# Numerators of the windowed attention: the low part is multiplied with the high part of the values only

## The chip, the cores and the metric

The kernel runs on one core of a Trainium2 chip. The core has a matrix engine (TensorE, here PE, with its weight loads shown apart as PEld), a vector engine (VectorE, DVE), a scalar engine (ScalarE, ACT), a general engine (GpSimd, POOL), and a queue engine (SyncE, SP) that issues nearly all of this kernel's transfers to 16 DMA engines. The metric is the device time of one execution in microseconds; a kernel's time is the median of its runs.

## The reference

One inference step of a one-layer decoder: a normalized input is projected into the parts of two mixers, a dilated sliding-window attention (8 heads of 64) and a gated linear attention (GLA, 4 heads), whose gated outputs go through one output projection. There are 2048 prompt tokens and 64 sample tokens (8 sequences of 8). The change touches the prompt's attention. Its three branches have the windows and dilations (128, 1), (512, 4) and (2048, 16); each is softmax attention over blocks of 128 queries, with the current and the previous block of 128 keys:

```python
DILATED = ((128, 1), (512, 4), (2048, 16))
BAND_BLOCK = 128

def softmax_attend(s, v, out_spec):
    m = jnp.max(s, axis=-1, keepdims=True)
    p = jnp.exp(s - m)
    den = jnp.sum(p, axis=-1)
    o = jnp.einsum(out_spec, p, v) / den[..., None]
    return o, m[..., 0] + jnp.log(den)

def dilated_branch_prompt(q, k, v, window, dil):
    ...
    s = jnp.einsum('brnqhd,brnkhd->brnqhk', qr, kk) * (hd ** -0.5)
    s = jnp.where(valid[None, None, :, :, None, :], s, -jnp.inf)
    o, lse = softmax_attend(s, vv, 'brnqhk,brnkhd->brnqhd')
    ...

def dilated_mixture(results):
    outs = jnp.stack([r[0] for r in results], axis=0)
    lses = jnp.stack([r[1] for r in results], axis=0)
    alpha = jax.nn.softmax(lses, axis=0)
    return jnp.einsum('gblh,gblhd->blhd', alpha, outs)
```

The numerators of the title are the sums of `p` times `v` before the division.

## The kernel before

**Numbers in two parts.** Products that need more than a 16-bit float holds are made of float16 pairs: a value is written as a high part (its rounding to float16) and a low part (the rest, again float16). In the input projections (`project`, L1761) three products are added: high by high, high by low, low by high. In the attention, the values of each head are stored with 64 high columns beside 64 low columns, so that a block of values for one head is a 128x128 tile; the exponentials `p` are split into a high and a low 128x128 block as well (`split`, L1003 to L1016).

**One unit of attention** is made by `attend` (L1018) from four steps. `pre` loads queries, keys and values. `qk` makes scores on PE (L1031, tiles `s`), then DVE adds the mask and finds the extreme (L1039) and ACT takes the exponential (L1042) into tiles `p`. `tr` transposes `p` in float32 through PE (L1049, tiles `t`), and `split` makes the two parts `pt`: one unit in two goes over ACT (L1008) and DVE (L1009), the others over ACT (L1011 and L1013) or DVE (L1015) and POOL (L1016). `pv` multiplies on PE: for each head `i` and each key block `b`, first the high part (`c` = 0) and then the low part (`c` = 1) of `pt` is loaded as weights, and the 128 columns of values are streamed through it into the PSUM tile `O` (L1064). The 128 columns of one head in `O` thus end as 64 columns of sums with the high values and 64 with the low values; `post` calls `added` (L1075 to L1081), in which ACT copies the second half out and DVE adds the first half to it. There are 600 such pairs of products, 1200 matmuls: two key blocks in most units of the branches of dilation 1 and 4 (`unit`), one in the branch of dilation 16 (`branch3`).

**What runs beside it.** From about 153 us to 735 us of the span these units are interleaved on PE with the projections of the input (values, queries, keys, then the GLA's query, key, value and gate blocks). Behind that come the GLA itself, the attention of the sample tokens, and the output projection (L2120). On POOL and DVE, dot products of the cached keys with the sample queries run beside the prompt's attention (L1616, L1617); their keys come in by DMA.

**Order.** The order of the instructions on every engine is written out: a table of numbers per engine, applied by `in_order` (L675), sets for each engine which instruction follows which. Waits between engines are semaphores that follow from the data.

Of the kernel before, what the change touches and what calls it, by code (L numbers as in the profile page):

```python
# [18 lines left out]
P = 128  # L19
# [3 lines left out]
HD = 64  # L23
# [667 lines left out]
def tile_hymba(ctx: ExitStack, tc: tile.TileContext, A: dict):  # L691
# [277 lines left out]
    with ExitStack() as c1:  # L969
# [33 lines left out]
        def split(out, in_, f):  # L1003

            split_[0] += 1
            h, l = out
            if split_[0] % 2:
                ACT.activation(h, in_, AF.Copy, scale=P_SCALE)  # L1008
                DVE.scalar_tensor_tensor(l, in_, P_SCALE, h, ALU.mult, ALU.subtract)  # L1009
            else:  # L1010
                ACT.activation(f, in_, AF.Copy, scale=P_SCALE)  # L1011
                if split_[0] % 4:
                    ACT.activation(h, f, AF.Copy)  # L1013
                else:
                    DVE.tensor_copy(h, f)  # L1015
                POOL.tensor_tensor(l, f, h, ALU.subtract)  # L1016

        def attend(tag, nh, nb, scores, mask, vf, nmf, denf, OT, pre=None, post=None, neg=-1.0):  # L1018

            w = nb * P
            t = {}

            def qk():
                s_ps = ps_S.tile([P, 512], F32, name=f"s_{tag}", tag="S")
                s = t["s"] = sp.tile([P, 512], F32, name=f"p_{tag}", tag="s")
                for i in range(nh):
                    prods = scores(i)
                    for n, (q, k) in enumerate(prods):  # L1030
                        PE.matmul(  # L1031
                            s_ps[:, i * w : (i + 1) * w], q, k,
                            start=(n == 0), stop=(n == len(prods) - 1),
                        )
                    if nh == 2 or i % 2:
                        yield
                for i in range(nh):
                    sl = slice(i * w, (i + 1) * w)
                    DVE.tensor_tensor_reduce(  # L1039
                        s[:, sl], s_ps[:, sl], mask, neg, BIG, ALU.add, ALU.min, nmf(i)  # L1040
                    )
                    ACT.activation(  # L1042
                        s[:, sl], s[:, sl], AF.Exp, bias=nmf(i), scale=-1.0, accum_out=denf(i)
                    )

            def tr():
                p_ps = ps_P.tile([P, 512], F32, name=f"t_{tag}", tag="PT")
                for i in range(nh * nb):
                    PE.transpose(  # L1049
                        p_ps[:, i * P : (i + 1) * P], t["s"][:, i * P : (i + 1) * P], ident[:]  # L1050
                    )
                    if i == 1:
                        yield
                pt = t["pt"] = ptp.tile([P, 2, 512], F16, name=f"pt_{tag}", tag="pt")
                w_ = slice(0, nh * w)
                split([pt[:, c, w_] for c in range(2)], p_ps[:, w_], t["s"][:, w_])
                yield

            def pv():
                for i in range(nh):  # L1060
                    o_ = OT(i)
                    for n in range(2 * nb):
                        b, c = divmod(n, 2)
                        PE.matmul(  # L1064
                            o_, t["pt"][:, c, (i * nb + b) * P : (i * nb + b + 1) * P], vf(i, b),
                            start=(n == 0), stop=(n == 2 * nb - 1),
                        )
                    if nh == 2 or i % 2:
                        yield
                if post:  # L1070
                    post()

            return [pre, qk, tr, pv]
# [602 lines left out]
        for nm_, src in (("q", A["q_norm_w"]), ("k", A["k_norm_w"])):  # L1676
            i = "qk".index(nm_)
# [210 lines left out]
        for i in range(3):  # L1888
            for lst, nm_ in ((st["qbd"], "qbd"), (Sbd, "Sbd"))[: 2 if i < 2 else 1]:
                t = gst.tile([P, 2, 256], F32, name=f"{nm_}{i}")  # L1890
# [644 lines left out]
```

## Time and profile before

| | us |
|---|---|
| median of 3 runs | 1231.39 (1228.66 to 1232.98) |
| the profiled execution, its own time | 1232.75 |
| its span, first to last instruction | 1230.7 |
| DVE busy in the span | 916.5 |
| ACT busy in the span | 826.2 |
| POOL busy in the span | 539.2 |

The profile shows one execution. An engine's busy time is the union of its instructions' times; a group of instructions is shown by source line, with count, busy time and the mean duration of one. The matmul's duration runs from its start to its modelled end, and several matmuls are under way at once, so durations of matmuls can't be added up: from the start of one to the start of the next is less. A chain of waits follows the work back from the last instruction and shows for each piece how far the time advanced; for a run of matmuls that is start to start. A weight load (PEld) stands in a row of its own and lies beside the matmuls.

### The profile page before, as it was taken

What the parts mean: (1) busy time and instruction counts of PE and PEld (TensorE: products, weight loads), DVE (VectorE), ACT (ScalarE), POOL (GpSimd) and SP (SyncE); (2) the same over time, 40 slices, a digit from 0 to 9 for tenths busy, and PEclk for the clock granted to TensorE, in tenths of its full rate; (3) what the DMA queues carried; (4) which work ended last, traced back from release to release, by engine and by line L of the source; (5) the groups of instructions that cost most, each with busy time, mean ns of one, the idle gap of its engine ahead of it and who ended that gap; (6) DMA issues with size and microseconds to landing.
All of it is one profiled execution on the core that took longest, in us unless ns stands there. A gap on an engine that the chain in (4) does not pass through costs nothing.

```text
span 1230.7 us, 26121 instructions
## 1 busy us (share of the span) xinstructions
PE 1174.5 (95%) x8942; PEld 717.4 (58%) x8942; DVE 916.5 (74%) x2457; ACT 826.2 (67%) x2189; POOL 539.2 (44%) x478
## 2 busy tenths in 40 slices
PE   3899999999999899998999999999999999999998
PEld 1444475566566556765777676645546665555543
DVE  5888687888878957777778665678888999743562
ACT  7656598789779968987777554577788864521220
POOL 0054444565547335553354467755544454311220
PEclk9999999999999999999999999999999999999999
DMA  7488956777955897799999978956673287999962
GB/s 260 161 235 217 235 186 152 204 218 193 228 175 169 202 270 220 258 241 284 275 245 265 250 232 222 267 167 224 223 227 103 95 266 254 320 367 403 385 223 77
DMA packets 235832, 283.07 MB, mean 230 GB/s; under 512 B 116194, under 2 KB 146867, under 8 KB 232627
## 3 DMA queue, kind: packets, MB, share of 16 engines
q1 hardware_dynamic: 235698, 281.40, 76.7%
q8 instruction: 71, 1.16, 0.4%
q14 instruction: 63, 0.51, 0.1%
HBM read 183.02 MB, written 75.24 MB: 210 GB/s over the span
## 4 chain that ended last, share of the span: by engine, by line
PE 45%; DVE 8%; ACT 4%; DMA 3%; issue 2%; POOL 1%; SPq 1%; ACTq 0%; POOLq 0%; DVEq 0%
PE Y L2120 11%; PE acc_g L1761 6%; PE acc_vb L1761 5%; PE acc_qkb L1761 4%; PE acc_gb L1761 4%; PE OS L2377 2%; PE O L1064 2%; PE t L1049 2%; PE s L1031 2%; PE sc_e L875 1%; DMA o_d<-o 1%; PE tm L2085 1%; DVE kq_e L846 1%; DVE Sbd L1940 1%; ACT qbd L834 1%
## 5 line engine op out<-in xcount | busy, mean ns | idle before, releaser
L1761 PEld LDWEIGHTS <-hr 128*128 128x128 f16 x1824 | 171.4, 98 | 103.5 <-issue 12.0
L1616 POOL TENSOR_TENSOR pr<-k,qb 128x512 f32<-128x512 f32 x128 | 169.0, 1320 | 142.3 <-DVE sck L1617 81.3
L1042 ACT ACTIVATE p<-p,o 128x256 f32<-128x256 f32 (+1 forms) x384 | 173.6, 455 | 23.6 <-DVE o L1039 21.1
L2120 PE MATMUL Y<-w_o,mh 128*128 128x512 f16 x768 | 187.7, 379 | 0.2 <-DVE xr L2127 0.2
L1761 PEld LDWEIGHTS <-hl 128*128 128x128 f16 x1248 | 117.7, 98 | 103.9 <-issue 5.0
L1064 PE MATMUL O<-v,pt 128*128 128x128 f16 x1200 | 172.5, 220 | 5.7 <-DVE pt L1009 1.7
L1016 POOL TENSOR_TENSOR pt<-p,pt 128x512 f16<-128x512 f32 (+1 forms) x80 | 91.6, 1145 | 148.5 <-ACT pt L1013 83.3
L1049 PE MATMUL t<-ident,p 128*128 128x128 f32 x600 | 135.3, 278 | 3.4 <-ACT p L1042 3.1
L1064 PEld LDWEIGHTS <-pt 128*128 128x128 f16 x1200 | 105.7, 99 | 49.8 <-POOL pt L1016 4.6
L1761 PE MATMUL acc_g<-w_g,hr 128*128 128x272 f16 (+1 forms) x768 | 118.7, 277 | 0.9 <-DVE so_g L1303 0.6
L1761 PE MATMUL acc_v<-w_v,hl 128*128 128x512 f16 x384 | 112.0, 382 | 1.9 <-DVE vp L1416 0.9
L1617 DVE TENSOR_REDUCE sck<-pr 128x8 f32<-128x512 f32 x128 | 87.1, 681 | 35.7 <-POOL pr L1616 35.2
L2120 PEld LDWEIGHTS <-mh 128*128 128x128 f16 x768 | 71.1, 98 | 69.3 <-issue 3.1
L1761 PE MATMUL acc_q<-w_q,hl 128*128 128x512 f16 x384 | 110.6, 379 | 0.0
L1031 PE MATMUL s<-kk,qq 128*128 128x256 f16 (+1 forms) x512 | 106.5, 264 | 3.9 <-DVE o L1039 2.2
L1761 PE MATMUL acc_k<-w_k,hl 128*128 128x512 f16 x384 | 109.7, 379 | 0.0
L1039 DVE CUSTOM_DVE_ANT_0 p<-s,m3w,scl_s 128x128 f32<-128x128 f32 (+1 forms) x256 | 90.7, 394 | 19.9 <-PE s L1031 10.4
L1761 PE MATMUL acc_vb<-w_vb,hr 128*128 128x512 f16 x384 | 102.2, 379 | 0.0
L1761 PE MATMUL acc_gb<-w_gb,hr 128*128 128x512 f16 x384 | 96.4, 380 | 0.1
L1049 PEld LDWEIGHTS t<-ident,p 128*128 128x128 f32 x600 | 78.1, 141 | 28.5 <-ACT p L1042 8.3
L1761 PE MATMUL acc_qkb<-w_qkb,hr 128*128 128x512 f16 x288 | 85.1, 379 | 0.0
L2162 POOL TENSOR_TENSOR oc<-oc 128x512 f32<-128x512 f32 x32 | 36.3, 1152 | 101.7 <-DVE oc L2155 96.0
(546 smaller groups left out, 2512.5 us busy)
## 6 DMA issues: line engine op xcount, KB each, us to landing
k<-in_cache_k_win SPq DMA_DIRECT2D x104, 256.0 KB
sv_b<-in_cache_v_win SPq DMA_DIRECT2D x24, 1024.0 KB
hr<-h_d SPq DMA_DIRECT2D x44, 512.0 KB
qb<-q_d SPq DMA_DIRECT2D x64, 256.0 KB
oc<-o_d SPq DMA_DIRECT2D x48, 264.0 KB
o_d<-o SPq DMA_DIRECT2D x64, 132.0 KB
x<-in_x_prompt SPq DMA_DIRECT2D x16, 512.0 KB
h_d<-hl SPq DMA_DIRECT2D x16, 512.0 KB
```

What stands on the lines that cost most here:

```text
L1016: POOL.tensor_tensor(l, f, h, ALU.subtract)
L1031: PE.matmul(s_ps[:, i * w : (i + 1) * w], q, k, start=(n == 0), stop=(n == len(prods) - 1),)
L1039: DVE.tensor_tensor_reduce(s[:, sl], s_ps[:, sl], mask, neg, BIG, ALU.add, ALU.min, nmf(i))
L1042: ACT.activation(s[:, sl], s[:, sl], AF.Exp, bias=nmf(i), scale=-1.0, accum_out=denf(i))
L1049: PE.transpose(p_ps[:, i * P : (i + 1) * P], t["s"][:, i * P : (i + 1) * P], ident[:])
L1064: PE.matmul(o_, t["pt"][:, c, (i * nb + b) * P : (i * nb + b + 1) * P], vf(i, b), start=(n == 0), stop=(n == 2 * nb - 1),)
L1616: POOL.tensor_tensor(pr[:], kt, qt, ALU.mult)
L1617: DVE.tensor_reduce(out, pr[:].rearrange("p (u k d) -> p u k d", u=2, k=4), AX.X, ALU.add)
L1761: PE.matmul(z, a_[:, k, :], w[:, p_, k, cols], start=(k == 0 and i == 0), stop=(k == KT - 1 and i == 2),)
L2120: PE.matmul(Y[:], a_[:, k, :], w_[:, part, k, :512], start=(i == 0), stop=(i == len(prods) - 1),)
L2162: eng.tensor_tensor(o_[g], o_[g], w[:, g].unsqueeze(2).to_broadcast([P, NH, HD]), ALU.mult)
L2377: PE.matmul(OS[32 * x : 32 * x + 32, 0:256], ps(x), vs_[bb][:, 256 * u : 256 * u + 256], start=(i == 0), stop=(i == 13),)
```

## The change

The products of the low part of `pt` take only the first 64 columns of the values (the high ones) and add into only the first 64 columns of the head's part of `O`. What is left out is the product of the low part of `p` with the low part of `v`. The products of the high part are as before, and so are the weight loads, the splitting and `added`.

```diff
                     for n in range(2 * nb):
                         b, c = divmod(n, 2)
+                        d = slice(0, P - HD * c)
                         PE.matmul(
-                            o_, t["pt"][:, c, (i * nb + b) * P : (i * nb + b + 1) * P], vf(i, b),
-                            start=(n == 0), stop=(n == 2 * nb - 1),
+                            o_[:, d], t["pt"][:, c, (i * nb + b) * P : (i * nb + b + 1) * P],
+                            vf(i, b)[:, d], start=(n == 0), stop=(n == 2 * nb - 1),
                         )
```

The added line shifts the numbers of all lines behind it by one: L1064 becomes L1065.

No instruction is moved on any engine. On PE, an early place in the list of the branch of dilation 1 (a row has the line, the operation, and for a matmul the tile that it writes, the tiles that it reads, and contraction rows x moving columns; a transpose of L1049 stands in one row with its weight load) reads before:

```order
L1761 MATMUL acc_q_2360<-w_q,hl_1190 128x512
L1064 LDWEIGHTS pt_0_0_0_1_1289
L1064 MATMUL O_0_0_0_1320<-v_0_0_0_1229,pt_0_0_0_1_1289 128x128
L1064 LDWEIGHTS pt_0_0_0_1_1289
L1064 MATMUL O_0_0_0_1320<-v_0_0_0_1229,pt_0_0_0_1_1289 128x128
L1049 MATMUL t_0_0_2_0_1411<-ident,p_0_0_2_0_1340 128x128
```

and now:

```order
L1762 MATMUL acc_q_2360<-w_q,hl_1190 128x512
L1065 LDWEIGHTS pt_0_0_0_1_1289
L1065 MATMUL O_0_0_0_1320<-v_0_0_0_1229,pt_0_0_0_1_1289 128x128
L1065 LDWEIGHTS pt_0_0_0_1_1289
L1065 MATMUL O_0_0_0_1320<-v_0_0_0_1229,pt_0_0_0_1_1289 128x64
L1049 MATMUL t_0_0_2_0_1411<-ident,p_0_0_2_0_1340 128x128
```

Only the second product of the pair is narrower; what follows it here is a transpose, whose weights are float32. A later place on PE, in the units of the fourth block of queries (tiles `O_3_...`), read before:

```order
L1064 LDWEIGHTS pt_3_1_1_0_7647
L1064 MATMUL O_3_1_1_7708<-v_2_1_1_5939,pt_3_1_1_0_7647 128x128
L1064 LDWEIGHTS pt_3_1_0_1_7597
L1064 MATMUL O_3_1_0_7617<-v_2_1_0_5825,pt_3_1_0_1_7597 128x128
L1761 LDWEIGHTS hr_7473
L1761 MATMUL acc_qkb_8022<-w_qkb,hr_7473 128x512
```

and reads now:

```order
L1065 LDWEIGHTS pt_3_1_1_0_7647
L1065 MATMUL O_3_1_1_7708<-v_2_1_1_5939,pt_3_1_1_0_7647 128x64
L1065 LDWEIGHTS pt_3_1_0_1_7597
L1065 MATMUL O_3_1_0_7617<-v_2_1_0_5825,pt_3_1_0_1_7597 128x128
L1762 LDWEIGHTS hr_7473
L1762 MATMUL acc_qkb_8022<-w_qkb,hr_7473 128x512
```

Here the narrower product is followed by a weight load of float16, as most are: in the whole list, 600 matmuls of `O` have become 128x64, 75 of them stand ahead of a float32 transpose of L1049, and the rows of DVE, ACT, POOL and SP are as before.

## The prediction

> **What bounds the kernel now.** I read the page first, for the engine that has no room:
>
> ```profile
> PE 1174.5 (95%) x8942; PEld 717.4 (58%) x8942; DVE 916.5 (74%) x2457; ACT 826.2 (67%) x2189; POOL 539.2 (44%) x478
> PE   3899999999999899998999999999999999999998
> PEclk9999999999999999999999999999999999999999
> ```
>
> PE is busy for 95% of the span, nowhere below 8 tenths after the first slice, and at nearly full clock. A busy share of matmuls says little by itself, since they overlap. So the next question is what one matmul costs from start to start. The groups by shape give durations, and the chain of waits gives the advance of runs of matmuls (start, length, number):
>
> ```profile
> L1064 PE MATMUL O<-v,pt 128*128 128x128 f16 x1200 | 172.5, 220 | 5.7 <-DVE pt L1009 1.7 <-DVE o L1081 1.5 <-POOL pt L1016 1.4
> L1761 PE MATMUL acc_q<-w_q,hl 128*128 128x512 f16 x384 | 110.6, 379 | 0.0
> 583.57 0.28 PE O L1064 x5
> 544.61 1.73 PE acc_qkb L1761 x8
> ```
>
> A product of `O` lasts 220 ns by its row, but five in a row advance the time by 0.28 us, 56 ns each; eight products of 512 columns advance it by 1.73 us, 216 ns each. The difference, 160 ns for 384 columns, is 0.417 ns per column, and 128 columns then explain 53 of the 56 ns: what is paid for is the stream of moving columns, with about 3 ns on top, and the weight load of each product lies beside the matmul ahead of it. The durations of the groups say the same: (379 - 220) / 384 is 0.414 ns per column.
>
> Then the stages. The table by stretches has, for all engines and below for L1064 alone, stretch, length, busy time and count of PE, PEld, DVE, ACT, POOL, then clock, DMA share, GB/s:
>
> ```profile
> 153.00:200.00 47.00, 44.47 (x405) 31.47 (x404) 40.08 (x147) 46.95 (x162) 18.70 (x18) 1.00 0.53 172
> 200.00:350.00 150.00, 148.43 (x1045) 92.63 (x1042) 120.43 (x311) 117.99 (x325) 86.34 (x66) 1.00 0.80 208
> 350.00:450.00 100.00, 92.47 (x729) 61.88 (x728) 78.81 (x220) 87.54 (x251) 46.23 (x35) 1.00 0.75 193
> 450.00:550.00 100.00, 98.84 (x808) 68.94 (x807) 75.84 (x236) 89.59 (x268) 52.81 (x44) 1.00 0.80 238
> 550.00:735.00 185.00, 178.26 (x1491) 126.57 (x1489) 137.89 (x445) 128.14 (x421) 85.22 (x69) 0.99 0.98 261
> 735.00:950.00 215.00, 208.05 (x1606) 123.12 (x1605) 166.13 (x399) 148.52 (x356) 122.54 (x124) 1.00 0.67 206
> 950.00:1231.00 281.00, 274.38 (x2235) 151.43 (x2231) 181.00 (x445) 111.66 (x231) 81.14 (x77) 1.00 0.73 264
> ...
> 153.00:200.00 47.00, 20.20 (x146) 12.35 (x146) 1.00 0.53 172
> 200.00:350.00 150.00, 46.42 (x287) 26.58 (x286) 1.00 0.80 208
> 350.00:450.00 100.00, 32.56 (x256) 21.27 (x256) 1.00 0.75 193
> 450.00:550.00 100.00, 38.75 (x264) 23.84 (x264) 1.00 0.80 238
> 550.00:735.00 185.00, 34.52 (x251) 21.66 (x249) 0.99 0.98 261
> ```
>
> Three kinds of stretch are to be seen. In 200 to 350 and 450 to 550 PE is idle for 1.6 and 1.2 us only: PE sets the pace. In 153 to 200 ACT is busy for 46.95 of 47 us, and in 350 to 450 PE is idle for 7.5 us with ACT at 87.5: there PE shares the pace with ACT and what stands behind it. In 550 to 735 the DMA engines are at 0.98. Who ends PE's waits from 153 to 735, and what the chain of waits consists of in the last two of these stretches:
>
> ```profile
> PE s L1031 <- DVE o L1039: 4.0, 3, 1.7
> PE t L1049 <- ACT p L1042: 3.1, 8, 0.9
> PE O L1064 <- DVE pt L1009: 1.7, 2, 1.5
> ...
> by line: PE acc_qkb L1761 47.8%; PE t L1049 14.7%; PE O L1064 14.0%; PE s L1031 13.1%; DVE w_g L1285 1.7%; issue 1.5%; DVE p L1039 0.9%; ACT p L1042 0.6%; DVE o L1081 0.3%; PE mx_g L1206 0.3%; DVE o L1039 0.1%; PE mx_g L1203 0.1%
> ...
> by line: PE acc_g L1761 25.5%; PE acc_vb L1761 22.4%; DMA o_d<-o 6.8%; PE O L1064 5.8%; PE s L1031 4.4%; PE t L1049 4.4%; DMA T_q<-qp_d 4.3%; DVE p L1039 3.1%; DMA ga_d<-so_g 2.9%; ACT p L1042 2.8%; issue 1.9%; SPq L1574 1.8%; DVE T_q L1479
> ```
>
> From 450 to 550 the chain runs over PE for 89.6% (47.8 + 14.7 + 14.0 + 13.1), 14% of it over the products that the change touches. From 550 to 735 PE has 62.5% (25.5 + 22.4 + 5.8 + 4.4 + 4.4); transfers, DVE and ACT have much of the rest.
>
> **The change, part by part.** Nothing is moved or added, and no wait of weight changes. The one edit takes 64 of 128 columns from 600 of the 1200 matmuls of L1064. A product of 64 columns costs 56 - 64 x 0.417 = 29.3 ns from start to start, if the columns are what is paid for: 26.7 ns less. 600 x 26.7 ns = 16.0 us is the most that the edit can give.
>
> The first deduction is the weight load of the next matmul. It was hidden behind 56 ns and has to fit behind 29. No row shows a matmul that short ahead of a full weight load, so this is bounded from the loads' rows (duration last before the bar's second part):
>
> ```profile
> L2377 PEld LDWEIGHTS OS<-sv_b,P3x 128*32 128x32 f32 x256 | 8.3, 110 | 5.8 <-issue 0.4 <-DMA out_y_prompt<-xr 0.4
> L875 PEld LDWEIGHTS sc_e<-qbd,kq_e 128*64 128x64 f32 x768 | 27.3, 137 | 20.3 <-issue 11.4 <-POOL kq_e L842 4.7 <-ACT qbd L834 1.7
> L1933 PEld LDWEIGHTS O<-vb,full 128*128 128x128 f32 x128 | 20.8, 191 | 3.2 <-issue 0.3
> L1049 PEld LDWEIGHTS t<-ident,p 128*128 128x128 f32 x600 | 78.1, 141 | 28.5 <-ACT p L1042 8.3 <-ACT p L1011 1.7 <-issue 0.9
> L1064 PEld LDWEIGHTS <-pt 128*128 128x128 f16 x1200 | 105.7, 99 | 49.8 <-POOL pt L1016 4.6 <-DVE pt L1009 4.1 <-issue 3.1
> L1761 PEld LDWEIGHTS <-hr 128*128 128x128 f16 x1824 | 171.4, 98 | 103.5 <-issue 12.0
> ```
>
> Float32 loads of 32, 64 and 128 columns last 110, 137 and 191 ns: 27 ns for 32 columns more and 54 ns for 64 more, so 0.84 ns per column on a fixed latency of 83 ns. If that latency holds for all loads, a float16 load of 98 ns keeps the array's weight side for about 15 ns, and the transposes' load of 141 ns for about 58 ns. Both lie hidden behind a 56 ns product today. Behind 29 ns the first still fits and the second does not. By the order of PE, 75 of the 600 narrow products stand ahead of a transpose; those I count as giving nothing (their bounds are 0 and 26.7 ns each, 2.0 us in all). That leaves 525 x 26.7 ns = 14.0 us, or 23.4 ns for each of the 600 on the mean. The bounds of the float16 case are 26.7 ns each and nothing; I take the first, by the row of 98 ns, and keep the second as a rival.
>
> The second deduction is by stage. Half of the counts of L1064, times 23.4 ns:
> - 200 to 350, 143 products, 3.4 us. PE has no idle time to speak of: all of it on the path.
> - 450 to 550, 132 products, 3.1 us. The chain runs over PE for nine tenths: 2.8 us.
> - 153 to 200, 73 products, 1.7 us, and 350 to 450, 128 products, 3.0 us. Here ACT's exponentials (L1042), DVE's row (L1039) and the split release PE. Each of these starts from an earlier product of PE, so a faster PE also releases them sooner, but ACT has no room in the first. Bounds nothing and 4.7; I take half, 2.35 us.
> - 550 to 735, 125 products, 2.9 us. PE's share of the chain, 62.5%: 1.8 us. Bounds nothing, if transfers set the pace, and 2.9.
>
> The sum is 3.4 + 2.8 + 2.35 + 1.8 = 10.35 us. What is shortened in one stage must also pass through the later ones. In the stretches up to 550 the DMA engines stand at 0.80 or less on the mean, so that the transfers for the next stretch can start earlier by the 8.5 us that PE is then ahead; behind 735 PE is idle for only 7 of 215 and 7 of 281 us and DMA is at 0.67 and 0.73, so I let the lead go through whole. What is late next: ACT's exponentials in 153 to 200 and 350 to 450, and the transposing gathers T_q and T_k of the third branch after 550. ACT's copies and DVE's additions of `O` (L1080, L1081) come sooner and cost the same.
>
> The profiled execution took 1232.75 us (span 1230.7 and 2.05 around it): it becomes 1222.4. The median of the runs shown, 1231.39, is 1.4 us lower: **1221.0 us** is the forecast.
>
> The Trainium skill (TensorE: Matmul & The Clock Gate, section Back-to-back issue gap) gives about 81 ns per matmul of 128 columns in a sustained stream of load and matmul pairs, set by both instructions. The trace does not agree: the run of five above has 56 ns each. By that page the pair and not its columns would be paid for, and the sum would be near nothing, which is the first rival's result.
>
> **The rivals.**
> *The weight load is the floor.* The 56 ns could be the load's own pace and not the columns': no pair in this trace is faster, and 128 weight columns at 0.417 ns are 53 ns too. Then every narrow product still waits for the next load, and nothing is gained: 1231. Against it stands that loads of 141 and of 98 ns hide behind the same 56 ns, so that the faster one should leave some 43 ns over. The Trainium skill (TensorE: Matmul & The Clock Gate, section Weight-path perf modes) says that the fast weight load for 128 columns that aren't float32 was measured at about twice the plain load, and its section on LDWEIGHTS puts the plain load at columns / 1.2 GHz: an estimate from both is 53 ns, this rival's result. The measured 98 and 141 ns speak against that figure, as above. No row settles it. Chance 0.08.
> *The lead is lost at others.* ACT in 153 to 200 and 350 to 450 sets the pace alone, and the DMA engines at 0.98 let only half of the lead into 735. Then the 2.35 and 1.8 us are gone and half of the remaining 6.2 us: 3.1 us gained, 1228. For it: the DMA share, and transfers on the chain, the longest below. Against it: PE is idle for 6.7 of 185 us there. Chance 0.17; from case to case 1225 to 1230, so that I count half of it as faster.
> *All of it arrives.* Every wait starts from PE and moves with it, and the transposes' loads hide as well: 14.0 to 16.0 us, 1215.4 to 1217.4. Chance 0.17.
> *Slower, by the clock.* One wait of the third branch let the clock drop:
>
> ```profile
> 564.09 7.89 DMA T_q<-qp_d
> 572.38 0.38 PE L1449 MATMUL acc_vb_s<-w_vb,hs 128*128 128x512 f16 x1 [2.05 <-ACT w_vb L1284]
> 570.00:575.00 5.00, 2.45 (x17) 1.54 (x15) 4.01 (x12) 4.95 (x14) 0.57 (x1) 0.83 1.18 255
> 575.00:580.00 5.00, 5.00 (x39) 3.65 (x37) 4.94 (x11) 4.00 (x9) 0.00 (x0) 0.82 0.90 278
> ```
>
> Here a gather of 7.89 us and then PE idle for 2.05 us were followed by a granted clock of 0.83 and 0.82 in two stretches of 5 us, 0.17 x 5 + 0.18 x 5 = 1.75 us of PE's time. If the lead turns into idle time in front of such gathers, the lead is lost and each further gap costs another 1.75 us. With three of them the time is 1231.4 + 5.2 = 1237; it is slower than before by more than can be told (3.7 us, 0.3%) from the third on. Against it: in all of the busy stretches the clock stands at 1.00, and DMA can start ahead. Chance 0.05.
> *The edit does less than it says* is excluded: the order has 600 matmuls of 64 columns.
>
> **How the numbers follow.** The forecast's own case, 6.2 us (nothing from the shared stages) to about 13 us gained, 1218 to 1225, has 0.53. With the rivals: 0.17 for all of it, 0.17 for the lost lead, 0.08 for the load's floor, 0.05 for slower. About 0.3% (3.7 us) is what a measurement of this kernel can tell from no change. Faster: 0.53 + 0.17 + half of 0.17, 0.79. Within: the other half and 0.08, 0.16. Slower: 0.05. The range goes from 1215, the full 16.0 us, to 1230, the end of the lost lead; it leaves out the floor and the slower case, 0.13, and some of the edges.
>
> **What would show it.** In the profile after: runs of `O` in the chain of waits that advance by about 43 ns per product on the mean instead of 56; the products' mean duration near 206 ns (half of them 27 ns shorter); no added idle time before transposes; span near 1220; PE's idle time up by about 4 us in 153 to 200, 350 to 450 and 550 to 735. The forecast is wrong if runs still advance by 56 ns (the load's floor), or if they are shorter and PE's idle time between 153 and 735 grows by 10 us or more (lost lead), or if the clock falls in more places than before.

## The result and the profile after

The changed kernel takes 1228.13 us, the median of 20 runs (1222.92 to 1231.92); the kernel before, timed beside it, 1231.61 us, the median of 20. The ratio is 0.9973, with a 95% interval of 0.996 to 0.9986: 3.5 us or 0.27% faster. That is a gain that the interval tells from nothing, just inside the 0.3% that the prediction called no change, inside the range of 1215 to 1230, and a third of the 10.35 us forecast. One of the 20 executions of the kernel before was a slow one (1369.15 us) and is not in the ratio.

The profiled execution of after took 1224.72 us, with a span of 1222.9. It is 3.4 us under its kernel's median, while the profiled one of before (1232.75) was 1.1 us above its own. The two profiles therefore differ by 8.0 us, the medians by 3.5, and a difference between single executions can't be read as the change's worth. What can be read in one pair is how the instructions follow each other.

From the page of after, busy time, then the slices of PE and the granted clock:

```profile
PE 1168.8 (96%) x8942; PEld 704.6 (58%) x8942; DVE 915.3 (75%) x2457; ACT 825.3 (67%) x2189; POOL 540.0 (44%) x478
PE   3999999999999889998999999999999999999998
PEclk9899999999999999999999999999999999999999
```

PE's busy time fell by 5.7 us only (1174.5 before), though 16 us of columns are gone, and one slice shows a clock of 8 tenths where before had none (it lies from 31 to 61 us, ahead of the first product that the change touches). The groups by shape of after, the products first, then the weight loads that the prediction bounded (busy time, mean ns of one, then idle time ahead and what ended it):

```profile
L1065 PE MATMUL O<-v,pt 128*128 128x128 f16 x600 | 112.1, 220 | 1.6 <-DVE o L1082 1.1 <-ACT pt L1008 0.3
L1065 PE MATMUL O<-v,pt 128*128 128x64 f16 x600 | 100.4, 193 | 3.9 <-POOL pt L1016 1.9 <-DVE pt L1009 1.8
L1049 PEld LDWEIGHTS t<-ident,p 128*128 128x128 f32 x600 | 77.9, 141 | 32.2 <-ACT p L1042 12.1 <-ACT p L1011 2.0 <-issue 1.2
L1065 PEld LDWEIGHTS <-pt 128*128 128x128 f16 x1200 | 100.9, 99 | 51.6 <-POOL pt L1016 7.2 <-DVE pt L1009 4.5 <-issue 3.5
```

A product of 64 columns lasts 193 ns against 220: 27 ns less, as forecast. The weight loads last what they did, and there is more idle time ahead of them: before the transposes' loads 32.2 us against 28.5, of it 12.1 for ACT's `p` against 8.3. The table by stretches of after, for all engines (columns as in the prediction):

```profile
153.00:200.00 47.00, 44.03 (x403) 30.16 (x401) 39.93 (x146) 46.92 (x163) 19.48 (x19) 1.00 0.53 174
200.00:350.00 150.00, 148.41 (x1060) 90.51 (x1059) 122.52 (x319) 119.69 (x332) 86.49 (x66) 1.00 0.80 209
350.00:450.00 100.00, 91.51 (x721) 58.89 (x720) 77.94 (x215) 86.54 (x247) 46.18 (x35) 0.98 0.76 199
450.00:550.00 100.00, 99.41 (x831) 67.37 (x830) 75.48 (x239) 91.43 (x273) 55.93 (x45) 1.00 0.79 237
550.00:735.00 185.00, 178.46 (x1511) 125.45 (x1510) 137.25 (x447) 127.66 (x421) 86.56 (x72) 1.00 0.98 267
```

The second, fourth and fifth stretch hold more matmuls than before (1060 against 1045, 831 against 808, 1511 against 1491), and PE is still called busy for the same time: from 153 to 735 us its idle time is 20.2 us, and was 19.5. The busy share hides the loss, since a matmul's record lasts 193 or 220 ns and covers a shorter gap up to the next one's start.

Both kernels issue the same 8942 matmuls in the same order, so the time between the same two matmuls can be compared, which is sharper than fixed stretches. The table gives these lengths in us between the matmuls that stood at the stretch's ends in before, from two profiles of before and three of the changed kernel. In brackets is the time in them at which the clock was granted at half rate.

| stretch | before | before_again | after | after_again | after_third | forecast gain |
|---|---|---|---|---|---|---|
| 153 to 200 | 47.03 | 47.04 | 46.81 | 46.83 | 46.79 | 0.85 |
| 200 to 350 | 149.98 | 149.22 | 148.19 | 148.17 | 148.55 | 3.4 |
| 350 to 450 | 100.05 | 101.46 [3.4] | 101.06 [3.4] | 100.39 [6.8] | 100.91 [3.4] | 1.5 |
| 450 to 550 | 99.88 | 98.94 | 97.26 | 96.84 | 98.65 | 2.8 |
| 550 to 735 | 185.05 [3.4] | 183.79 | 181.54 | 186.28 [3.4] | 182.21 | 1.8 |
| 153 to 735 | 582.0 | 580.4 | 574.9 | 578.5 | 577.1 | 10.35 |

With half of the bracketed time taken off (what PE lost in it at most), 153 to 735 takes 580.3 and 578.7 us before and 573.2, 573.4 and 575.4 after: 5.5 us less on the means. So at full clock about half of the forecast arrived, and some of that is paid back in clock. The experiments are about these two losses.

### The profile page after: what moved, and what is told of

The parts are those of the page before. It is cut to its first block, busy times and chain, and to the rows that moved or that the text cites. A ratio compares the mean times of both kernels' runs of the same rounds, so it can differ in the third digit from the quotient of the medians.

```text
span 1222.9 us, 26121 instructions
## 1 busy us (share of the span) xinstructions
PE 1168.8 (96%) x8942; PEld 704.6 (58%) x8942; DVE 915.3 (75%) x2457; ACT 825.3 (67%) x2189; POOL 540.0 (44%) x478
## 5 line engine op out<-in xcount | busy, mean ns | idle before, releaser
L1042 ACT ACTIVATE p<-p,o 128x256 f32<-128x256 f32 (+1 forms) x384 | 173.8, 456 | 24.3 <-DVE o L1039 16.8
L1065 PE MATMUL O<-v,pt 128*128 128x128 f16 (+1 forms) x1200 | 157.4, 206 | 5.6 <-POOL pt L1016 1.9
L1049 PE MATMUL t<-ident,p 128*128 128x128 f32 x600 | 136.9, 282 | 4.0 <-ACT p L1042 3.5
L1065 PEld LDWEIGHTS <-pt 128*128 128x128 f16 x1200 | 100.9, 99 | 51.6 <-POOL pt L1016 7.2
L1049 PEld LDWEIGHTS t<-ident,p 128*128 128x128 f32 x600 | 77.9, 141 | 32.2 <-ACT p L1042 12.1
```

The source lines that it names most:

```text
L1042: ACT.activation(s[:, sl], s[:, sl], AF.Exp, bias=nmf(i), scale=-1.0, accum_out=denf(i))
L1049: PE.transpose(p_ps[:, i * P : (i + 1) * P], t["s"][:, i * P : (i + 1) * P], ident[:])
L1065: PE.matmul(o_[:, d], t["pt"][:, c, (i * nb + b) * P : (i * nb + b + 1) * P], vf(i, b)[:, d], start=(n == 0), stop=(n == 2 * nb - 1),)
```

## The experiments

Theory **W** says that the freed time of PE turns into new waits on ACT, DVE and POOL, whose chains don't get shorter by as much. Theory **C** says that PE, less busy with columns, is granted a lower clock. Theories **D** and **E** came later: D, that DVE and POOL with the dot products of the window are the takers of the freed time; E, that no single engine is. "Pooled" below are the means over the timed executions of a kernel with their standard errors, and the mean of the granted clock that stands beside each execution's time. The 130 of before leave out those of the first comparison, which have no clock on record, and the 9 beside the dot products:

| kernel | executions | mean us | against before | mean clock |
|---|---|---|---|---|
| before | 130 | 1232.24 ± 0.19 | | 0.9961 |
| the change | 44 | 1228.98 ± 0.40 | -3.3 ± 0.4 | 0.9945 |
| light_before | 12 | 1231.48 ± 0.40 | -0.8 ± 0.4 | 0.9954 |
| light_after | 13 | 1225.67 ± 0.62 | -6.6 ± 0.7 | 0.9955 |
| narrow_13 | 12 | 1228.84 ± 0.61 | -3.4 ± 0.6 | 0.9960 |
| narrow_02 | 13 | 1231.58 ± 0.70 | -0.7 ± 0.7 | 0.9948 |
| narrow_branch3 | 12 | 1231.10 ± 0.73 | -1.1 ± 0.8 | 0.9960 |
| narrow_133 | 19 | 1228.68 ± 0.50 | -3.6 ± 0.5 | 0.9960 |
| most_64 | 12 | 1228.55 ± 0.91 | -3.7 ± 0.9 | 0.9937 |
| order_before | 12 | 1231.12 ± 0.56 | -1.1 ± 0.6 | 0.9956 |
| order_after | 18 | 1227.36 ± 0.59 | -4.9 ± 0.6 | 0.9954 |
| order_133 | 12 | 1228.72 ± 0.81 | -3.5 ± 0.8 | 0.9954 |
| dots_before | 5 | 1226.40 ± 0.54 | -5.8 ± 0.6 | 0.9966 |
| dots_after | 5 | 1221.14 ± 0.97 | -11.1 ± 1.0 | 0.9970 |

**Both kernels again**, unchanged, for more executions and for profiles that can be set beside the first ones.

> The kernel before, once more, for its clocks and a second profile. Theory W (the missing 7 us of gain went into new waits of PE on ACT, DVE and POOL between 153 and 550 us): its granted clocks are like those of the changed kernel, near 0.995 on the mean. Theory C (the changed kernel falls into half-rate stretches more often, each of 3.4 us costing 1.7 us): clocks of this kernel near 0.998, of the changed one near 0.9945, a difference that is worth 3 to 4 us.

> The changed kernel, once more, beside the kernel before on the same chip: 3 to 4 us faster by both theories. Theory W: in its profile the lead of PE over the kernel before grows in 200 to 350 us by about 1.8 us where the narrower products free 3.8 us. Theory C: the lead grows by nearly 3.4 us there wherever the clock is full, and is lost at the stretches of half rate.

Measured: 1229.5 and 1229.27 us, medians of 12 each beside 1232.18 for before; ratios 0.999 (0.9974 to 1.0006) and 0.9987 (0.9969 to 1.0004). This pair alone couldn't tell the kernels apart; their mean clocks are 0.9966 and 0.9933. What the two profiles of one kernel share is no accident of one execution. A matmul's slot is priced here by its columns: 2.7 ns and 0.417 ns for each (56 ns for 128 columns, 216 for 512), twice that per column for float32. PE's time beyond the sum of its slots between 153 and 735 (half-rate time left out) is 33 to 35 us in both of before and 44 to 45 in both of after: 10 us more wait. At 45 places both profiles of after wait over 60 ns longer than either of before, 5.1 us in all, and at 43 of these they agree to 0.1 us. Runs of products in the chain of waits of after_again (start, length, number):

```profile
708.01 0.14 PE O L1065 x3
720.50 0.20 PE O L1065 x5
729.34 0.31 PE O L1065 x7
```

Seven products advance by 0.31 us, 44 ns each, where before has 0.39 for seven (56 each). The slots are as the forecast has them; the loss is between the runs.

**A lighter copy.** ACT's copy of half of `O` and DVE's addition are what free the buffer of `O`; here ACT copies one column, which DVE adds to all, in both kernels:

```diff
-            ACT.activation(l[:], o4[:, :, 1], AF.Copy)
-            DVE.tensor_tensor(out, o4[:, :, 0], l[:], ALU.add)
+            ACT.activation(l[:, :, 0:1], o4[:, :, 1, 0:1], AF.Copy)
+            DVE.tensor_tensor(
+                out, o4[:, :, 0], l[:, :, 0:1].to_broadcast([P, 4, HD]), ALU.add
+            )
```

> The kernel before, with ACT's copy out of O (L1080) cut from 64 columns per head to one, which DVE adds to all 64: leaves out the sums with the low values except for one column; ACT has some 20 us less to do between 153 and 735 us. Theory W: 2 to 6 us faster than before, since ACT ends some of PE's waits. Theory C: within 2 us of before.

> The changed kernel with the same lighter copy (leaves out the same sums). Theory W: the gain of the narrower products over the kernel with the light copy alone is larger than the 3.5 us of the change, about 6 to 10 us, because ACT gives way. Theory C: the gain stays at 3 to 4 us and goes with the clocks.

> The changed kernel with the lighter copy of O, once more, since only seven of its runs were compared: leaves out the sums with the low values except for one column. Theory W: 6 us faster than before or more, as the first time. If the first time was chance: 3 to 4 us, as the change.

Measured: light_before 1231.37 us, ratio 0.9993 (0.9979 to 1.0007); light_after 1225.16, 0.9946 (0.9927 to 0.9966), and again 1226.65, 0.9948 (0.9932 to 0.9964). ACT is busy for 17 us less in both (809.2 and 807.8 against 826.2 and 825.3 us), and before gains nothing from it that these runs can tell. On the lighter copy the change is worth 5.8 ± 0.7 us (pooled) instead of 3.3 ± 0.4. In this pair the clock doesn't differ (0.9954 and 0.9955), while between the plain kernels it falls by 0.0016, which is 1.9 us of 1229 at most. So much of the difference of 2.5 us could be the clock's. PE's time beyond its slots from 153 to 735 still grows here, from 34 us to 42 and 45, so the copies are not shown to be what takes the freed time.

**The narrow products in some places only.** The first three kernels narrow the second and fourth block (234 to 345 and 454 to 545 us), the first and third (154 to 236 and 352 to 443), and the third branch (543 to 727); narrow_133 is the first and the last of these together:

```diff
-                        d = slice(0, P - HD * c)
+                        d = slice(0, P - HD * c if nh == 2 and tag[2] in "13" else P)
...
-                        d = slice(0, P - HD * c)
+                        d = slice(0, P - HD * c if nh == 2 and tag[2] in "02" else P)
...
-                        d = slice(0, P - HD * c)
+                        d = slice(0, P - HD * c if nh == 4 else P)
...
-                        d = slice(0, P - HD * c)
+                        d = slice(0, P if nh == 2 and tag[2] in "02" else P - HD * c)
```

> Only the units of the second and fourth block of 512 queries have narrow low products (256 of 600, 6.8 us of columns; they lie in 230 to 350 and 454 to 546 us, where PE was hardly idle); the other low products keep 128 columns. Theory W (freed columns reach the end only where PE sets the pace, less the float32 loads and new waits of PE): 3.5 to 5 us faster than before, as fast as the whole change or faster. Theory C (the loss comes with more stretches of half rate, which follow the gaps of 153 to 200 and 350 to 450 us): the clock stays near that of before, 0.996, and the gain is 4.5 to 6 us.

> Only the units of the first and third block have narrow low products (216 of 600, 5.8 us of columns, in 154 to 236 and 352 to 443 us, where PE waits for ACT, DVE and POOL). Theory W: 0 to 1.5 us faster than before. Theory C: the clock falls toward that of the whole change, 0.994 to 0.995, and the time is within 1 us of before on either side.

> Only the third branch has narrow low products (128 of 600, 3.4 us of columns, in 543 to 727 us, where the DMA engines are at 0.98). Theory W: 0 to 2 us faster. Theory C: clock as before, and 2 us or more faster.

> Narrow low products in the second and fourth block and in the third branch (384 of 600); those of the first and third block keep 128 columns. By the single parts, 3.7 and 1 us: 4 to 5 us faster than before, so 1 us faster than the whole change, with a clock near 0.996 as before (theory C: the first and third block lower the clock and give nothing). If the parts don't add: as the change, 3 to 3.5 us.

> The narrow low products without those of the first and third block, once more (seven runs so far). Theory C (the 216 narrow products of those blocks bring under 1 us and lower the clock): 1 to 2 us faster than the change beside it, clock near 0.996. If the first time was chance: within 0.7 us of the change, clock near 0.994.

Measured: narrow_13 1228.26 us, ratio 0.9974 (0.9957 to 0.9991); narrow_02 1231.51, 0.9996 (0.9984 to 1.0007); narrow_branch3 1230.81, 0.9992 (0.9977 to 1.0007); narrow_133 1227.32, 0.996 (0.9945 to 0.9975), and again 1229.95, 0.9974 (0.9961 to 0.9987). 256 of the 600 products, those in the two stretches where PE is hardly ever idle, give as much as all of them. Of the 6.8 us (256 x 26.7 ns) that they free, half arrives, at a clock equal to before's. The 216 products of the first and third block free 5.8 us, give 0.7 ± 0.7 and lower the clock to 0.9948: that part of the change is as good as spent on waits and clock. The 128 of the third branch free 3.4 us and give 1.1 ± 0.8. Leaving the first and third block out (narrow_133) is no better than the change, though, against what theory C had for it; why is not shown.

**Still fewer columns.** Here every product behind the first of its group has 64 columns, which frees another 5.8 us:

```diff
-                        d = slice(0, P - HD * c)
+                        d = slice(0, HD if n else P)
```

> A larger dose: besides the low products, the high products of the second key block take 64 columns too (816 of 1200 narrow, another 5.8 us of columns freed; leaves out the product of the high part of p with the low part of v for that block). Theory W: 1 to 2.5 us faster than the change. Theory C: the clock falls below that of the change, to 0.993 or less, and takes about 1 us back.

Measured: 1228.42 us, ratio 0.9971 (0.9954 to 0.9988): nothing more than the change, with the lowest clock of all, 0.9937. Its profile has five stretches of 3.41 us at half rate (at 197, 341, 405, 446 and 573 us), where before has one or two. By theory W alone there should have been a third to a half of 5.8 us. In this one profile it is there at full clock: with half of its half-rate time taken off, 153 to 735 takes 571.8 us against 574.0 on the mean of the change, and the clock takes it back.

**PE's order around the waits.** In PE's list of orders the next one to three projection products were pulled ahead of a waiting `s`, `t` or `O` at 23 places (the edit is in the table of numbers alone); order_133 has this order and narrow_133's slice.

> The changed kernel with another order on PE: at 23 places between 153 and 735 us where PE waits for ACT, DVE or POOL over 60 ns longer than in the kernel before (5.9 us at 37 places in both profiles, 4.2 us of it covered here), the next one to three projection matmuls are taken ahead of the waiting instruction. Theory W, told closer (the list of PE leaves each unit's chain over DVE and ACT so many PE instructions of cover; narrower products make the same instructions a shorter cover, and the rest of the chain becomes a wait): 2 to 4 us faster than the change, 1225 to 1227. If the waits have another cause (ACT or DVE short of time as a whole): within 1 us of the change.

> The kernel before, all products of 128 columns, with the same new order. Theory W: the cover was enough there, so the order gives nothing: within 1.5 us of before on either side. If the new order is better by itself: as much faster as for the changed kernel.

> The changed kernel with the new order on PE, once more. In its first profile the wait at the 37 places fell from 10.9 to 6.7 us, but PE's wait from 153 to 735 us as a whole stayed at 46.5 us beside 44 and 45 us, so theory W as told for that run should have given nothing; its six runs were 3 us faster than the change all the same, with a clock of 0.9967. If the waits are only pushed on: within 1 us of the change here. If the order does pay, by cover or by fewer stretches of half rate: 2 to 3 us faster than the change again, the latter with a clock near 0.996.

> The new order on PE with the narrow products of the second and fourth block and of the third branch only. If both gains are real and differ in place: 6 to 8 us faster than before, the fastest of all. If the new order only works through the clock, which narrow_133 keeps anyway: as narrow_133 or within 1 us of it.

Measured: order_after 1226.12 us, ratio 0.9944 (0.9927 to 0.9961), and again 1228.38, 0.9964 (0.9947 to 0.9981); order_before 1231.0, 0.9985 (0.9973 to 0.9998); order_133 1228.99, 0.9968 (0.9952 to 0.9983). The first reading, of 6 executions, was partly luck, as the second, of 12, shows. At the 37 places where the change waits longer than before, the waits fell from 10.9 to 6.7 us in sum, but PE's time beyond its slots from 153 to 735 did not fall (46.4 us against 43.9, 44.5 and 46.2 with the old order): what is taken off one wait comes back at a later one. Pooled it is 1.6 ± 0.7 us faster than the change. It is the fastest whole kernel of these, but with order_133 no better than narrow_133, whether the order pays stays open.

**The change a third time**, beside the last repeats:

> The changed kernel a third time, as the measure for the three kernels beside it: 3 to 3.5 us faster than before, clock near 0.994 (32 runs so far: 0.9942; 95 of before: 0.9960).

Measured: 1228.77 us, ratio 0.9973 (0.9959 to 0.9986), what the first comparison gave.

**Shorter dot products on POOL and DVE.** POOL's products over the window and DVE's sums of them are cut from 512 to 64 columns in both kernels, which takes 124 us from POOL and 75 from DVE:

```diff
-            POOL.tensor_tensor(pr[:], kt, qt, ALU.mult)
+            POOL.tensor_tensor(pr[:, :64], kt[:, :64], qt[:, :64], ALU.mult)
...
-                out, pr[:].rearrange("p (u k d) -> p u k d", u=2, k=4), AX.X, ALU.add
+                out, pr[:, :64].rearrange("p (u k d) -> p u k d", u=2, k=4), AX.X, ALU.add
```

> The kernel before, with the sample dot products (POOL L1616, DVE L1617) cut from 512 columns to 64: leaves out seven eighths of each sample score; the loads are as before. POOL has some 125 us and DVE some 70 us less to do between 232 and 828 us, and DVE waits less for POOL in its list. Theory D (DVE, held up by its dot products, and POOL end the new waits of PE): 3 to 8 us faster than before already. Theory E (no single engine: waits move from one place of the list to the next, as with the new order): 0 to 3 us.

> The changed kernel with the same short dot products (the same part left out). Theory D: its gain over the kernel with the short dot products alone is much larger than the 3.3 us of the change, 7 to 12 us, and PE's new wait from 200 to 550 us (about 6 us by the profiles) falls to 3 or less. Theory E: the gain stays at 2 to 5 us and the new wait at 5 to 6.

Measured: 1225.95 us, ratio 0.9947 (0.9932 to 0.9962), and 1221.29, 0.9911 (0.9895 to 0.9928), of 5 executions each: the change is worth 4.7 us by medians, 5.3 ± 1.1 by means, and the clocks are alike (0.9966 and 0.9970). The shorter dot products alone gain 5.8 us, as D had it and not E (0 to 3). But by the times between the same matmuls that gain lies from 550 to 735 (179.7 us against 183.4 and 183.8 in before, half of the half-rate time taken off) and from 735 to 950 (213.4 against 215.0 and 215.1), and not in the stages where the forecast had its largest terms. Had DVE and POOL been the takers of the freed time (D), PE's new wait should have gone. PE's time beyond its slots from 200 to 550, half-rate time left out, grows from 16.8 to 23.2 us here, as it does without the cut (15.6 and 17.5 to 20.7, 23.4 and 25.1). The views of PE's weight side's waits from 153 to 735 (engine, line, releaser: us, times, longest) show who is waited for, first in before, then in after, then in the pair with the cut:

```profile
PEld t L1049 <- ACT p L1042: 8.3, 21, 1.1
PEld L1761 <- issue: 7.5, 8, 2.2
PEld L1064 <- POOL pt L1016: 4.6, 8, 1.5
PEld L1064 <- DVE pt L1009: 4.1, 8, 1.9
```

```profile
PEld t L1049 <- ACT p L1042: 12.1, 32, 1.1
PEld L1762 <- issue: 10.3, 19, 2.3
PEld L1065 <- POOL pt L1016: 7.2, 11, 1.6
PEld L1065 <- DVE pt L1009: 4.5, 10, 1.9
```

```profile
PEld t L1049 <- ACT p L1042: 6.5, 18, 1.1
PEld L1064 <- POOL pt L1016: 5.6, 8, 1.5
PEld L1761 <- issue: 4.4, 4, 2.2
PEld L1064 <- DVE pt L1009: 2.8, 6, 1.3
```

```profile
PEld t L1049 <- ACT p L1042: 9.8, 25, 1.1
PEld L1065 <- POOL pt L1016: 6.1, 9, 1.6
PEld L1762 <- issue: 5.2, 8, 2.3
PEld L1065 <- DVE pt L1009: 4.1, 6, 2.5
```

In both pairs the wait for ACT's `p` grows by two fifths to a half in time and count (21 to 32, 18 to 25) with the longest unchanged at 1.1 us, and each of the other rows grows as well, among them "issue", for which the profile shows no releaser. These are new short waits on several engines, not one longer wait on one. D is out as the taker, and E is what is left; no run relieves several engines at once.

## Why the forecast was three times the gain

**(a) The slots were right.** At the median the next matmul starts 28 ns behind a narrow product and 56 behind a wide one; the forecast had 29.3 and 56. The rival of the weight load as a floor is out: a pair of a full float16 load and a matmul goes at 28 ns. By the Trainium skill (TensorE: Matmul & The Clock Gate, section Back-to-back issue gap) a sustained stream of loads and matmuls stands at about 81 ns for 128 columns, and columns / 2.4 + 2.5 ns (an estimate of 29.2 ns for 64) holds for an isolated matmul only. The trace disagrees with the first: the second describes the pairs here.

**(b) The transposes' deduction was right.** The same instructions in time order, start and length, in before and then in after:

```profile
546.94 0.33 PE L1064 MATMUL O<-v,pt 128*128 128x128 f16 x3
547.11 0.28 PE L1049 MATMUL t<-ident,p 128*128 128x128 f32 x1
547.23 0.28 PE L1064 MATMUL O<-v,pt 128*128 128x128 f16 x2
547.34 0.28 PE L1049 MATMUL t<-ident,p 128*128 128x128 f32 x1
547.45 0.22 PE L1064 MATMUL O<-v,pt 128*128 128x128 f16 x1
```

```profile
544.26 0.28 PE L1065 MATMUL O<-v,pt 128*128 128x64 f16 x3
544.38 0.31 PE L1049 MATMUL t<-ident,p 128*128 128x128 f32 x1
544.52 0.25 PE L1065 MATMUL O<-v,pt 128*128 128x128 f16 x2
544.60 0.31 PE L1049 MATMUL t<-ident,p 128*128 128x128 f32 x1
544.74 0.22 PE L1065 MATMUL O<-v,pt 128*128 128x128 f16 x1
```

Three products advance the time by 0.17 us before and 0.12 after, two by 0.11 and 0.08. But a transpose now takes 0.14 us up to the next start, where it took 0.12 and 0.11. Its load doesn't fit behind 28 ns, and the delay shows one slot later than expected, in the transpose's own slot and not ahead of it: 143 ns at the median of the 75 places, where it was 116, and 109 behind other matmuls. A product and its transpose thus take 28 + 143 = 171 ns, and took 56 + 116 = 172: nothing is gained there. Less the 109, both leave some 62 ns for the load, an estimate close to the prediction's 58. The sum of what the 75 slots take beyond 109 ns grows from 0.7 to 2.7 us: 2.0 us, as deducted.

**(c) The stages failed, and this is the step that was wrong.** "200 to 350 ... PE has no idle time to speak of: all of it on the path" stood for 3.4 us, and 450 to 550 for 2.8, the largest terms of the sum; by the table of the same matmuls about 1.3 and 1.8 arrived (half of the half-rate time taken off). An idle time of 1 to 2 us was read as an engine with nothing to wait for. In truth the busy share could not show how close the others were: PE's instructions stand in one fixed order among chains through ACT, DVE and POOL, and those were only a little ahead of it. Of the 16.0 us freed 5.5 arrived at full clock, and PE's time beyond its slots took back the other 10.5: the 2.0 of the transposes and 8.5 of new waits, in all stages and on several releasers. Narrowing only these two stretches' products gave half of what was freed (narrow_13), so it holds where PE is busiest, too. In 153 to 200 the gain was 0.2 of 0.85 us, in 350 to 450 1.4 of 1.5, in 550 to 735 0.8 of 1.8; two profiles of one kernel differ by up to 3.0 us in the longer stretches, so only the first is sharp. Narrow_branch3, whose products are wide up to 543 us, takes 148.9 and 99.2 us in 200 to 350 and 450 to 550; with it in the mean of before, 1.1 and 1.8 us arrived there.

**(d) The lead goes through** was right: behind 735 nothing that was gained is lost; 735 to 950 takes 214.96 and 215.07 us before and 214.45, 214.39 and 214.55 after.

**The clock was a rival and became a term.** The forecast gave it 0.05 and a price of 1.75 us for each further drop, and looked for it in the gathers of the third branch. Drops came in other places, too. After_again from 404.6 to 411.4 us, then before and narrow_13 in the same two stretches (columns as above, the clock third from the end):

```profile
404.60:408.00 3.40, 2.04 (x23) 1.36 (x23) 3.40 (x11) 3.04 (x9) 1.81 (x1) 0.93 0.70 154
408.00:411.40 3.40, 3.40 (x22) 2.63 (x23) 3.37 (x12) 3.19 (x11) 0.50 (x1) 0.56 0.49 173
```

```profile
404.60:408.00 3.40, 2.28 (x25) 1.71 (x23) 3.40 (x8) 3.04 (x8) 1.44 (x1) 1.00 0.23 52
408.00:411.40 3.40, 2.81 (x27) 2.12 (x27) 3.40 (x14) 3.40 (x13) 0.37 (x1) 1.00 0.74 153
```

```profile
404.60:408.00 3.40, 2.01 (x23) 1.50 (x23) 3.40 (x9) 3.03 (x8) 1.81 (x1) 1.00 0.56 95
408.00:411.40 3.40, 3.08 (x32) 2.46 (x29) 3.36 (x14) 3.40 (x13) 0.00 (x0) 1.00 0.43 155
```

In the first, PE waits for DVE (1.4 us) and its weight side for POOL (1.6 us), with PE busy for 2.04 of 3.40 us; the clock falls to 0.56 for the next stretch, and 22 matmuls pass in it where before passes 27. Narrow_13, whose products are wide here, was busy for as little (2.01 us) and kept its clock. What differs is the columns: at 0.417 ns each (twice that for float32) they streamed for 0.38 of the 3.41 us ahead of the drop in after_again and for 0.42 of the same window in narrow_13. Of the 20 profiles, ten are of kernels with narrow products in the first and third block, and 7 of these have a half-rate stretch that begins between 197 and 199 or between 405 and 409 us. None of the ten with wide products there has one. So the narrow products do cost clock in those blocks. Between 153 and 735 us the three profiles of the change have 5 units of 3.41 us at half rate, 1.7 on the mean; the two of before have 2, 1.0 on the mean. Over the pooled executions the mean clock falls from 0.9961 to 0.9945, which is 1.9 us of 1229 if all of it is lost on PE's path. The executions' own spread says less: 0.001 of clock goes with 0.6 us among before's and 1.0 us among the change's, so 0.9 to 1.5 us for this fall. Where both kernels of a pair were granted the same clock (light, dots), the change was worth 5.8 ± 0.7 and 5.3 ± 1.1 us, as the 5.5 us of the same matmuls at full clock. So the books close nearly: 16.0 freed, 2.0 for the transposes, 8.5 for new waits, 1 to 2 for the clock, some 4 left, and 3.3 to 3.5 measured. The size of the clock's term is shown by these comparisons and by the correlation of time and clock among a kernel's executions (-0.63 in the change's), not by a run that changes the clock alone.

**Rivals.** "The lead is lost at others" (0.17, 1225 to 1230) named the right kind of loss, but put it in the wrong stages: it left 200 to 350 and 450 to 550 whole up to 735 us. That its 1228 is the measured time is luck. "All of it arrives" and the floor are out. The signs that the prediction set for itself tell it well, if they are read from start to start: 44 ns per product came as expected, while PE's wait from 153 to 735 grew by the 10 us that it had named as the sign of a lost lead. By the profile's idle time, which is what the prediction wrote, it grew by 0.7 us only, and the sign would have been missed. This rival should have had more than 0.17: PE takes its place in one order with three engines that pass work to it, and where PE had no idle time the prediction did not ask how far ahead these were.

**Open.** Which chain ends each new wait is not settled, nor whether the changed order pays, nor what beside the clock makes executions of one kernel differ by up to 16 us (1222.92 to 1239.22 among the 44 of the change).

## What to carry to other kernels

A busy share near 99% doesn't say that an engine is alone on the path: where it stands in a fixed order with others, only a third to a half of the freed time may arrive, as here, and the question for each stage is how far ahead of it the others are. Compare the same instructions' starts in two kernels, since busy time hides gaps shorter than an instruction's latency. Narrow a product where PE is the one that the others wait for; where it waits anyway, fewer columns give little time and may cost clock.

## What was not expected of the hardware

- A full float16 weight load of 128 x 128 and a matmul of 64 columns repeat every 28 ns: the load (recorded at 99 ns) is no floor at this size. A float32 load that doesn't fit lengthens the slot of its own matmul, from 116 to 143 ns here, and the recorded start ahead of it doesn't move.
- The clock falls to half in stretches of 3.41 us (also two or three in a row, 6.83 and 10.24), without PE being idle for as long: in the 20 profiles the longest gap ahead of one between 153 and 735 us was 0.9 to 3.4 us. What tells is how long columns streamed, counted as above. In each trace the clock's changes lie on one grid of 3.413 us. Of this grid's windows at full rate between 153 and 735 us, all 26 with a streamed share under 0.37 were followed by half rate, 5 of 8 from 0.37 to 0.385, 1 of 23 from there to 0.43, and none of some 3300 above. Of the two windows above, after_again's (0.38) lies in the narrow zone and narrow_13's (0.42) above it. The Trainium skill (TensorE: Matmul & The Clock Gate, section HAM oscillation) has as its rule that PE be idle for no more than about 3.4 us at a time; here shorter gaps within such a window were enough. The Trainium skill's section on a second HAM failure mode, on the same page, tells of frequent short idling with the same outcome, which these traces agree with.
